# Value rows of the context's experts gathered beside the latents' DeltaNet, from a queue of their own

## The chip, the cores and the metric

The program runs on one NeuronCore of a Trainium2. The metric is the device time of one execution in microseconds. The engines run in parallel, each in its own order: PE (TensorE, matmuls), DVE (VectorE), ACT (ScalarE), POOL (GpSimd, which issues the gathers here) and SP (which issues the other DMAs). They wait for each other by semaphores.

## The reference

A two-layer backbone over 512 latent tokens and 256 context tokens of width 1024. Layer 0 mixes tokens with a gated DeltaNet, layer 1 with attention; each is followed by product-key experts (`peer`), which pick 8 x 16 of 16384 experts for every token:

```python
def block_fn(xb):                      # 128 tokens
    ...
    idx = jnp.take_along_axis(cand_i, pos, axis=-1)      # 128 experts per token
    gate = jax.nn.softmax(best_s, axis=-1)
    act = jax.nn.gelu(jnp.einsum('pd,phkd->phk', xb, u_tab[idx]))
    coef = gate * act
    return jnp.einsum('phk,phkd->pd', coef, v_tab[idx])
...
for i in range(DEPTH):
    ...
    if i % 2 == 0:
        yc, yl = deltanet_mixer(hc, hl, ...)
    else:
        yc, yl = attention_mixer(hc, hl, ...)
    xl = xl + g1l * yl
    xl = xl + g2l * peer(norm(xl), ...)
    if not last:
        xc = xc + g1c * yc
        xc = xc + g2c * peer(norm(xc), ...)
return rmsnorm(xl, final_g)
```

In the DeltaNet the latents start from the state that the context leaves. The context reads nothing of the latents, and its experts' result is needed in layer 1's attention only.

## The kernel before, in words

The order of layer 0 is: the DeltaNet's projections, its steps for the context, the context's output projection and routing, then the DeltaNet of the latents (`dn_rec("l")`), their output projection (`dn_out("l")`), their routing, the table of gates (`gates_build`), a dense pass, and layer 1's attention.

`dn_rec("l")` works in four groups of two heads. A group prepares its chunks (kk, rp), inverts their triangular matrices together (`dn_inv`, in PSUM tiles mg), runs four steps per head and direction (`dn_step`: ks, yr, su, ops, each needing the state that the step before left), and transposes the result (tp), scaled by the gates zt. `dn_out("l")` adds up 16 heads in PSUM (po) for two blocks of 128 tokens at a time, evicts (y) and normalizes them.

Three of the four blocks of latents are not gathered: `dense` evaluates all experts for them, in 128 steps of matmuls (up, y). The fourth block of latents and both blocks of the context are gathered, one row of 128 x 1024 floats (512 KB) at a time, by indirect DMAs that POOL issues:

- `gather_u`: for each of 128 picks the rows of `u` for 128 tokens (L965), and the dot products with the tokens on DVE (L967). After 128 of them a block's coefficients are complete.
- `gather_v`: the values of 64 tokens of the context, one token at a time (L1017), and two matmuls (L1020) that add 128 rows, weighted, into a row of PSUM (yp). A half block is 64 of them, and there are four halves, 256 rows. Ahead of a half the picks and coefficients are transposed on PE (L1004).
- `gather_vt`: the values of the block of latents, summed on DVE (L984).

They share four buffers ("row"). All are generators in one list, `k.bg`. The loops of the main work call `tick(w)` at fixed places, with w from the table RATE, and tick runs a step of the list's first generator for each full unit of credit. So the list's order is the gathers' order: the dot products of the context (256, queued ahead of `dn_rec("l")`), three halves of the context's values (NVA = 3, queued after `dn_out("l")`), then, as routing of the fourth block ends, its dot products and values, and the fourth half. What is left runs in attention (`drain`), before the context is read. From the traced program a scheduler then writes each engine's order.

Of the kernel before, what the change touches and what calls it, by code (L numbers as in the profile page):

```python
# [18 lines left out]
P = 128  # L19
# [12 lines left out]
AHEAD = [i for r in (0, 2, 1, 3) for i in range(r, PK, 4)]      # blocks of experts, in the order of their evaluation ahead  # L32


class Kern:
    def __init__(self, ctx, tc, I, out, dbg):
        self.ctx, self.tc, self.nc, self.I, self.out, self.dbg = ctx, tc, tc.nc, I, out, dbg or {}
        nc = self.nc
        self.bg, self.credit = [], 0.0
        self.ug, self.ucredit, self.nu = None, 0.0, 0  # L40
# [13 lines left out]
    # gathers are issued in small steps between the other work  # L54
    def tick(self, w):
        self.credit += w
        while self.credit >= 1.0 and self.bg:
            self.credit -= 1.0
            try:
                next(self.bg[0])  # L60
            except StopIteration:
                self.bg.pop(0)
        if not self.bg:
            self.credit = 0.0

# [56 lines left out]
    def ada(self, l, r, pool=None):  # L122
        """chunks 2 * r and 2 * r + 1 of a layer's modulations, for latents (row 0) and context (row 1)"""
# [24 lines left out]
    def mod_rows(self, pool, l, s, sub, norm, nb=1, pool_g=None, **kw):  # L148
        """A = norm_g*(1+scale), S = shift, as rows on all partitions"""
# [10 lines left out]
    def norm_mod(self, pool, x, A, S, h):  # L160
        """h <- rmsnorm(x) * A + S"""
# [8 lines left out]
    def transp_split(self, pp, tag, h, hi, lo, b):  # L170
        """h [128, 1024] -> hi/lo[:, kb, b*128:...]"""
# [10 lines left out]
    # tokens on the free axis: 0..511 latents, 512..767 context  # L182
    def gate_math(self, p, pp, gx, n, G):
# [23 lines left out]
        # log1p(e) = ln(u) * e / (u - 1), or e where u rounds to 1  # L207
# [30 lines left out]
    def dn_in(self, G, later, ast, rec):  # L238
        """q, k, v, z and the gates; rec's first step is traced before the last heads, beside which it runs"""
# [67 lines left out]
    def dn_qkv(self, G, p, pp, pwp, hi, lo, wtile, heads, nb):  # L307
# [4 lines left out]
        W2 = TL + 4 + TC          # conv output span: latents, gap of 4, context  # L312
        XC = TL + 6               # start of the context in the padded row
# [83 lines left out]
    def dn_z(self, p, pp):  # L397
        """2 * silu(z)^T of the latents"""
# [24 lines left out]
    def dn_rec(self, seq, G, og_d, st_d):  # L423
# [5 lines left out]
        with ExitStack() as st:  # L429
# [8 lines left out]
            for g0 in range(0, QH, GR):  # L438
                pks, Pss, Us = [], [], []
                pg = p if g0 // GR % 2 else pq  # L440
                for hh in range(GR):
                    h = g0 + hh
                    Ps = pg.tile([P, MH, 2, P], F32, name="Pm", bufs=GR)
                    U = pg.tile([P, MH, 2, P], F32, name="U", bufs=GR)     # (c, v), dir
# [5 lines left out]
                    for c in range(n):  # L450
                        self.tick(self.rate[0])
                        kk = pqp.tile([P, 2, P], F32, name="kk")
                        nc.tensor.matmul(kk.rearrange("p a b -> p (a b)"), pk[:, c, 0, :],
                                         pk[:, c, 0:2, :].rearrange("p a b -> p (a b)"), start=True, stop=True)
                        km = pq.tile([P, 2, 2, P], F32, name="km", bufs=2)     # (kk, kq), dir
                        nc.vector.tensor_mul(km, kk.unsqueeze(2).to_broadcast([P, 2, 2, P]), self.tri.unsqueeze(1).to_broadcast([P, 2, 2, P]))
                        rp = pqp.tile([P, 2, 2, P], F32, name="rp")
                        ar = pq.tile([P, 2, 2, P], F32, name="ar", bufs=2)     # (v, dir)
# [116 lines left out]
    def dn_inv(self, p, pp, Us, MH, Z64):  # L575
        """Us[head][:, m, dir] <- (I + U)^-1, U triangular (upper for dir 0, lower for dir 1)."""
# [23 lines left out]
        R1 = t4("R1", [P, 2 * M, 32])     # rows of the inverses' transposes  # L600
        R2 = t4("R2", [P, 2 * M, 32])     # rows of the inverses
# [9 lines left out]
        # (source, target) blocks  # L611
        pairs = [[(0, 1), (2, 3)], [(1, 0), (3, 2)]]
        tp = pp.tile([P, M, 32], F32, name="mg")
# [5 lines left out]
        Tc = p.tile([P, M, 32], F32, name="Tc")  # L619
        nc.scalar.copy(Tc, tp)  # L620
        self.tick(self.rate[9])
        zp = pp.tile([P, M, 32], F32, name="mg")
# [7 lines left out]
        yp = pp.tile([P, M, 32], F32, name="mg")  # L630
# [13 lines left out]
        T6 = p.tile([P, M, 64], F32, name="T6")  # L644
        for mh in range(2):
            tp = pp.tile([P, 8, 64], F32, name="mg")
# [7 lines left out]
        for mh in range(2):  # L654
            yp = pp.tile([P, 8, 64], F32, name="mg")
# [12 lines left out]
    def dn_out(self, seq, og_d, xin, xout, put):  # L668
        """xout[b] = xin[b] + g1 * (o @ w_out); put(b, rows) for every finished block"""
# [4 lines left out]
        with tc.tile_pool(name="dno", bufs=1) as p, tc.tile_pool(name="dnop", bufs=1, space=PS) as pp:  # L674
# [4 lines left out]
            for b0 in range(0, n, 2):  # L679
                bs = range(b0, b0 + 2)  # L680
                ps = {(b, h): pp.tile([P, 512], F32, name="po", bufs=6 if n > 2 else 4) for b in bs for h in range(2)}
# [21 lines left out]
    def attention(self, xl, xc, order, rows, A0, gst, ost, pst):  # L703
        """(softmax(q k^T) v)^T of the latents, split, by heads; context is read after the gathers that finish it"""
# [533 lines left out]
def body(ctx, tc, I, out, dbg=None, upto=99):  # L1238
# [74 lines left out]
    for i in range(NVA):  # L1313
        vctx(i // 2, i % 2)
# [128 lines left out]
```

## Time and profile before

| | us |
|---|---|
| median of 3 runs (4876.7 to 4892.4) | 4885.92 |
| the profiled execution: span of its instructions | 4891.1 |
| PE busy | 4329.9 |
| DVE busy | 3587.0 |
| POOL busy | 1321.5 |

The profiled execution's own time is not among the runs by name; its span, from the first to the last instruction, lies 5.2 us above the median and 1.3 below the highest run. Busy times of different engines overlap. Most of the program is bound by PE; the stages that matter here are those between 940 and 3360 us of the span.

### The profile page before, as it was taken

How to read it: one execution, taken by the hardware profiler on the slowest of the kernel's cores; microseconds unless marked ns; L12 is line 12 of the kernel's file. 1: busy time of each engine (PE TensorE's matmuls, PEld its weight loads, DVE VectorE, ACT ScalarE, POOL GpSimd, SP SyncE). 2: the span in 40 equal slices, each digit the busy share in tenths (PEclk: the TensorE clock that was granted, in tenths of full speed). 3: DMA queues.
4: the chain of work that ended last, by engine and by line, in shares of the span. 5: the costliest groups of instructions: out<-in, count | busy, mean ns of one | idle time of the engine just before them, and what ended most of it. 6: DMA issues, size and time to landing. Idle time of an engine off the chain costs nothing. (4 is left out here: it accounts for less than half of the span.)

```text
span 4891.1 us, 68996 instructions
## 1 busy us (share of the span) xinstructions
PE 4329.9 (89%) x24564; PEld 3455.1 (71%) x24564; DVE 3587.0 (73%) x8483; ACT 1866.5 (38%) x3605; POOL 1321.5 (27%) x1111
## 2 busy tenths in 40 slices
PE   6999669757569698999999999988997999999998
PEld 3778547545444556666788888745687998888887
DVE  4667825899965857566688888645579888888886
ACT  2335553447450213344333333223333554333333
POOL 0000000134344433222333334440000102444441
PEclk8999789768679899999999999999999999999999
DMA  7744246447578877777999999872133678999996
GB/s 296 261 150 135 75 144 191 153 148 254 177 242 317 301 240 268 269 260 272 329 349 351 339 339 337 292 268 74 61 112 107 215 260 287 355 334 335 336 324 230
DMA packets 480616, 1196.55 MB, mean 245 GB/s; under 512 B 40752, under 2 KB 239152, under 8 KB 470416
## 3 DMA queue, kind: packets, MB, share of 16 engines
q1 hardware_dynamic: 332816, 655.21, 38.2%
q0 software_dynamic: 147456, 536.94, 31.5%
q8 instruction: 194, 3.18, 0.3%
q14 instruction: 150, 1.23, 0.1%
HBM read 1079.50 MB, written 112.49 MB: 244 GB/s over the span
## 5 line engine op out<-in xcount | busy, mean ns | idle before, releaser
L965 POOL DMA_INDIRECT row<-in_peer_u,idx x512 | 613.2, 1198 | 1513.3 <-DVE row L967 706.3
L100 PE MATMUL up<-hil,uh 128*128 128x384 f32 x2048 | 709.4, 346 | 44.7 <-ACT c L1094 44.1
L102 PE MATMUL up<-hil,ul 128*128 128x384 f32 x2048 | 697.2, 340 | 0.0
L101 PE MATMUL up<-lol,uh 128*128 128x384 f32 x2048 | 696.1, 340 | 0.0
L100 PE MATMUL y<-vh,ch 128*128 128x512 f32 x1536 | 602.8, 393 | 9.1 <-ACT ch L106 7.6
L101 PE MATMUL y<-vl,ch 128*128 128x512 f32 x1536 | 602.9, 393 | 0.0
L102 PE MATMUL y<-vh,cl 128*128 128x512 f32 x1536 | 508.8, 391 | 0.0
L981 POOL DMA_INDIRECT row<-in_peer_v,idx x256 | 339.9, 1328 | 456.3 <-DVE lhs L984 374.5
L100 PEld LDWEIGHTS up<-hil,uh 128*128 128x128 f32 x2048 | 386.9, 189 | 94.8 <-ACT c L1094 65.4
L106 ACT CAST uh<-ur 128x1024 fp32r<-128x1024 f32 x256 | 268.3, 1048 | 454.3 <-PE up L101 322.3
L1017 POOL DMA_INDIRECT row<-in_peer_v,iT x256 | 279.5, 1092 | 557.7 <-PE yp L1020 473.7
L107 DVE TENSOR_TENSOR vl<-vr,vh 128x1024 fp32r<-128x1024 f32 x256 | 312.9, 1224 | 127.1 <-ACT vh L106 125.1
L106 ACT CAST vh<-vr 128x1024 fp32r<-128x1024 f32 x256 | 268.6, 1051 | 359.9 <-PE y L102 325.0
L101 PEld LDWEIGHTS up<-lol,uh 128*128 128x128 f32 x2048 | 387.1, 189 | 19.2 <-issue 10.9
L102 PEld LDWEIGHTS up<-hil,ul 128*128 128x128 f32 x2048 | 386.5, 189 | 18.2 <-issue 15.1
L107 DVE TENSOR_TENSOR ul<-ur,uh 128x1024 fp32r<-128x1024 f32 x256 | 312.1, 1220 | 74.7 <-ACT uh L106 70.1
L967 DVE SCALAR_TENSOR_TENSOR row<-row,ghs 128x1024 f32<-128x1024 f32 x256 | 311.2, 1222 | 73.7 <-DMA row<-in_peer_u,idx 72.7
L1066 DVE TENSOR_SCALAR A<-iotar,kt 128x128 f32<-128x128 f32 x768 | 221.8, 289 | 174.4 <-PE gp L1068 171.9
L100 PEld LDWEIGHTS y<-vh,ch 128*128 128x128 f32 x1536 | 289.8, 189 | 70.3 <-ACT ch L106 9.1
L102 PEld LDWEIGHTS y<-vh,cl 128*128 128x128 f32 x1536 | 288.6, 188 | 64.6 <-issue 4.2
L984 DVE SCALAR_TENSOR_TENSOR lhs<-row,lcf,lhs 128x1024 f32<-128x1024 f32 x254 | 325.1, 1280 | 9.6 <-DMA row<-in_peer_v,idx 8.0
L101 PEld LDWEIGHTS y<-vl,ch 128*128 128x128 f32 x1536 | 290.1, 189 | 56.3 <-issue 2.5
(397 smaller groups left out, 8788.1 us busy)
## 6 DMA issues: line engine op xcount, KB each, us to landing
ur<-in_uT SPq DMA_DIRECT2D x256, 512.0 KB
vr<-in_peer_v SPq DMA_DIRECT2D x256, 512.0 KB
w<-in_ada_w SPq DMA_DIRECT2D x48, 1024.0 KB
G_d<-st SPq DMA_DIRECT2D x10, 4096.0 KB
gt<-G_d SPq DMA_DIRECT2D x64, 640.0 KB
act_d<-c SPq DMA_DIRECT2D x129, 192.0 KB
c<-act_d SPq DMA_DIRECT2D x129, 192.0 KB
wr<-in_dn_w_in SPq DMA_DIRECT2D x48, 512.0 KB
```

The source lines that it names most:

```text
L100: first = mm(ps, lh, rh, start=start, stop=False)
L101: mm(ps, lh, rl, start=False, stop=False)
L102: mm(ps, ll, rh, start=False, stop=stop)
L106: self.nc.scalar.copy(hi, src)
L107: self.nc.vector.tensor_sub(lo, src, hi)
L965: nc.gpsimd.indirect_dma_start(out=u, out_offset=None, in_=self.I["peer_u"], in_offset=bass.IndirectOffsetOnAxis(ap=ix[:, k:k + 1], axis=0))
L967: mv = nc.vector.scalar_tensor_tensor(u, u, 1.0, hs, op0=ALU.mult, op1=ALU.mult, accum_out=coef[:, k:k + 1])
L981: nc.gpsimd.indirect_dma_start(out=v, out_offset=None, in_=self.I["peer_v"], in_offset=bass.IndirectOffsetOnAxis(ap=ix[:, k:k + 1], axis=0))
L984: keep(nc.vector.scalar_tensor_tensor(y, v, coef[:, k:k + 1], y, op0=ALU.mult, op1=ALU.add))
L1017: nc.gpsimd.indirect_dma_start(out=v, out_offset=None, in_=self.I["peer_v"], in_offset=bass.IndirectOffsetOnAxis(ap=iT[:, t:t + 1], axis=0))
L1066: nc.vector.tensor_scalar(A, iota, kt[:, 0, t:t + 1], None, op0=ALU.is_equal)
```

## The change

A second list, `k.bgv`, holds the four halves of the context's values. `tick` runs it beside the first one, with credit of its own, and only while the first half's block stands in `summed`, where `gather_u` enters a block after its last dot product:

```diff
+        self.vcredit += w * self.vrate
+        while self.vcredit >= 1.0:
+            self.vcredit -= 1.0
+            if not (self.bgv and self.bgv[0][0] in self.summed):
+                self.vcredit = 0.0
+                break
+            try:
+                next(self.bgv[0][1])
+            except StopIteration:
+                self.bgv.pop(0)
...
         nc.scalar.activation(coef, coef, AF.Gelu)
         nc.vector.tensor_mul(coef, coef, gate.rearrange("p h k -> p (h k)"))
+        self.summed.add(j)
...
-NVA = 3         # halves of context blocks whose values are gathered before those of the latents
+VRATE = 1.0
```

The halves are queued before the latents' DeltaNet. After `dn_out("l")` what is left of them is moved to `k.bg`, ahead of the gathers of the latents; none comes after these:

```diff
+        gat.open_v(gst)
         for b in range(NX) if upto > 1 else ():
             gat.u(0, b, gate[1, b], idx[1, b])
+            for s in range(2):
+                gat.v_half(b, idx[1, b], (0, 1, 5), rows(xm_c, b), rows(xo_c, b), s)
+        k.vrate = VRATE
         for _ in k.dn_rec("l", G, og_l, st_d):
             pass
...
-    gat.open_v(gst)
     k.dense_open(lst, 0, ND, hi, lo)
-    vctx = lambda b, s: gat.v_half(b, idx[1, b], (0, 1, 5), rows(xm_c, b), rows(xo_c, b), s)
-    for i in range(NVA):
-        vctx(i // 2, i % 2)
+    k.vrate = 0.0
+    k.bg += [g for _, g in k.bgv]
+    k.bgv = []
...
     k.routing(0, hi, lo, TL, *lat, order, gathers)
-    for i in range(NVA, 2 * NX):
-        vctx(i // 2, i % 2)
...
-    k.drain(2 * NX - NVA)
+    k.drain()
```

The buffers of `gather_v` are so open during the DeltaNet, and others are made smaller: kk and mg share one PSUM bank, Tc and T6 one buffer, the latents' zt has two buffers in place of four, the latents' output projection five accumulators in place of six, and the copy cT falls away:

```diff
-                        kk = pqp.tile([P, 2, P], F32, name="kk")
+                        kk = pqp.tile([P, 2, P], F32, name="kk", tag="kk")
...
-        tp = pp.tile([P, M, 32], F32, name="mg")
+        tp = pp.tile([P, M, 32], F32, name="mg", tag="kk")
...
-        T6 = p.tile([P, M, 64], F32, name="T6")
+        T6 = p.tile([P, M, 64], F32, name="T6", tag="T6", bufs=1)
...
-                ps = {(b, h): pp.tile([P, 512], F32, name="po", bufs=6 if n > 2 else 4) for b in bs for h in range(2)}
+                ps = {(b, h): pp.tile([P, 512], F32, name="po", bufs=5 if n > 2 else 4) for b in bs for h in range(2)}
...
-        cT = pv.tile([P, P], F32, name="cT")
-        nc.vector.tensor_copy(cT, yp[:, 0:P])
...
-ZT = 8, 4
+ZT = 8, 2
```

Comments are taken out too, so line numbers after are some ten higher (L1031 after is L1020 before, L702 is L690, L997 is L984).

The first place is PE's order in the steps of the latents' last DeltaNet group. Before:

```order
L529 MATMUL ks<-S,pk 128x256 x2
L564 MATMUL ops<-vn,Pm 128x128 x2
L540 MATMUL yr<-pk,U 128x128
L529 MATMUL ks<-S,pk 128x256 x2
L541 MATMUL yr<-R,U 128x128
L540 MATMUL yr<-pk,U 128x128
L541 MATMUL yr<-R,U 128x128
L564 MATMUL ops<-vn,Pm 128x128 x4
```

and after, where `yp<-row,Cz` is a gathered value row of the context:

```order
L1031 MATMUL yp<-row,Cz 32x512 x2
L541 MATMUL ks<-S,pk 128x256 x2
L562 MATMUL su<-vd,pk 128x256
L576 MATMUL ops<-vn,Pm 128x128 x2
L552 MATMUL yr<-pk,U 128x128
L553 MATMUL yr<-R,U 128x128
L552 MATMUL yr<-pk,U 128x128
L553 MATMUL yr<-R,U 128x128
L1031 MATMUL yp<-row,Cz 32x512 x2
```

Before, no gathered value stood in this group; after, a pair of matmuls for one stands between one step and the next.

The second place is PE's order in the latents' output projection, from the last step on. Before:

```order
L564 MATMUL ops<-vn,Pm 128x128 x2
L513 MATMUL tp<-ident,o 128x128 x16
L690 MATMUL po<-W,o 128x512 x95
L176 MATMUL tr<-ident,fh 128x128 x8
L690 MATMUL po<-W,o 128x512 x11
L176 MATMUL tr<-ident,fh 128x128 x8
L690 MATMUL po<-W,o 128x512 x22
L1004 MATMUL yp<-ident,gcf_6341 128x128
L176 MATMUL tr<-ident,fh 128x128 x8
```

and after:

```order
L576 MATMUL ops<-vn,Pm 128x128 x2
L1031 MATMUL yp<-row,Cz 32x512 x4
L525 MATMUL tp<-ident,o 128x128 x16
L702 MATMUL po<-W,o 128x512 x26
L1031 MATMUL yp<-row,Cz 32x512 x2
L702 MATMUL po<-W,o 128x512 x3
L1031 MATMUL yp<-row,Cz 32x512 x2
L702 MATMUL po<-W,o 128x512 x4
L1031 MATMUL yp<-row,Cz 32x512 x2
L702 MATMUL po<-W,o 128x512 x26
L1031 MATMUL yp<-row,Cz 32x512 x2
```

Value rows now stand between the projection's matmuls (po), and before they began behind them, with the transposes of the coefficients (gcf).

The third place is DVE's order at the end of the dense pass, where lhs is the gathered block of latents and rt the dense blocks' results. Before (the first piece, and a little later the second):

```order
L984 SCALAR_TENSOR_TENSOR lhs_12955<-row,lcf_12956,lhs_12955 128x1024
L107 TENSOR_TENSOR vl<-vr,vh 128x1024
L984 SCALAR_TENSOR_TENSOR lhs_12955<-row,lcf_12956,lhs_12955 128x1024
L991 TENSOR_TENSOR lhs_12955<-lhs_12955,row 128x1024
L107 TENSOR_TENSOR ul<-ur,uh 128x1024
L1121 TENSOR_TENSOR c<-c,gt 128x320
L1122 TENSOR_TENSOR c<-c,st 128x64
L992 TENSOR_TENSOR lhs_12955<-lhs_12955,row 128x1024
```

```order
L1121 TENSOR_TENSOR c<-c,gt 128x320
L1122 TENSOR_TENSOR c<-c,st 128x64
L107 TENSOR_TENSOR cl<-c,ch 128x384
L1155 TENSOR_TENSOR rt__27332<-y_20097,dg_27328 128x512
L1155 TENSOR_TENSOR rt__27332<-y_20098,dg_27328 128x512
L1156 TENSOR_TENSOR rt__27332<-rt__27332,rx 128x512
L1155 TENSOR_TENSOR rt__27340<-y_20099,dg_27328 128x512
L1156 TENSOR_TENSOR rt__27332<-rt__27332,rx 128x512
```

and after:

```order
L997 SCALAR_TENSOR_TENSOR lhs_13120<-row,lcf_13121,lhs_13120 128x1024
L119 TENSOR_TENSOR cl<-c,ch 128x384
L997 SCALAR_TENSOR_TENSOR lhs_13120<-row,lcf_13121,lhs_13120 128x1024 x3
L1166 TENSOR_TENSOR rt__27324<-y_20604,dg_27320 128x512
L1166 TENSOR_TENSOR rt__27324<-y_20605,dg_27320 128x512
L1166 TENSOR_TENSOR rt__27332<-y_20606,dg_27320 128x512
L1166 TENSOR_TENSOR rt__27332<-y_20607,dg_27320 128x512
L997 SCALAR_TENSOR_TENSOR lhs_13120<-row,lcf_13121,lhs_13120 128x1024
L1167 TENSOR_TENSOR rt__27324<-rt__27324,rx 128x512 x2
L1167 TENSOR_TENSOR rt__27332<-rt__27332,rx 128x512 x2
L997 SCALAR_TENSOR_TENSOR lhs_13120<-row,lcf_13121,lhs_13120 128x1024 x3
```

Before, the latents' gathered values were complete ahead of the last dense steps; after, the last of them stand behind the first evictions of the dense results.

## Rows read from the trace of the kernel before

**Rows 1.** The page's first lines: span, then busy time and instructions of each engine

```profile
span 4891.1 us, 68996 instructions
...
PE 4329.9 (89%) x24564; PEld 3455.1 (71%) x24564; DVE 3587.0 (73%) x8483; ACT 1866.5 (38%) x3605; POOL 1321.5 (27%) x1111
```

**Rows 2.** Windows of six stages: engine busy us (instructions), TensorE clock, DMA share, GB/s

```profile
core 0: us, PE busy (x) PEld busy (x) DVE busy (x) ACT busy (x) POOL busy (x), PEclk, DMA share, GB/s
940.00:1285.00 345.00, 201.51 (x2220) 159.24 (x2222) 316.59 (x749) 199.96 (x635) 128.59 (x113) 0.69 0.59 198
1285.00:1450.00 165.00, 120.81 (x1190) 99.90 (x1186) 133.43 (x308) 104.57 (x369) 74.70 (x67) 0.82 0.65 216
1450.00:1627.00 177.00, 120.68 (x295) 55.54 (x294) 105.97 (x174) 9.36 (x17) 84.06 (x70) 0.82 0.87 310
1627.00:2332.00 705.00, 660.90 (x3449) 455.63 (x3449) 468.50 (x1824) 236.35 (x306) 233.92 (x211) 0.98 0.78 267
2332.00:3183.00 851.00, 849.13 (x4062) 726.57 (x4062) 672.07 (x974) 294.65 (x395) 330.11 (x281) 1.00 0.92 334
3183.00:3360.00 177.00, 145.15 (x614) 83.75 (x610) 81.39 (x187) 47.99 (x153) 63.29 (x64) 0.90 0.60 206
```

**Rows 3.** Windows of three stages, PE records of L1020 alone: PE, PEld, clock, DMA

```profile
1627.00:2332.00 705.00, 188.40 (x740) 25.96 (x740) 0.98 0.78 267
2332.00:3183.00 851.00, 24.77 (x100) 3.47 (x100) 1.00 0.92 334
3183.00:3360.00 177.00, 43.91 (x188) 6.06 (x184) 0.90 0.60 206
```

**Rows 4.** PE timeline in routing: start us, us, operation, records

```profile
1799.69 0.33 PE L101 MATMUL up<-lol,uh 128*128 128x384 f32 x1
1799.95 1.05 PE L1020 MATMUL yp<-row,Cz 128*32 128x512 f32 x4
1800.93 0.44 PE L102 MATMUL up<-hil,ul 128*128 128x384 f32 x1
1801.21 0.33 PE L100 MATMUL up<-hil,uh 128*128 128x384 f32 x1
1801.38 0.34 PE L101 MATMUL up<-lol,uh 128*128 128x384 f32 x1
```

**Rows 5.** PE timeline at the end of the dense pass, two value rows

```profile
3182.44 1.05 PE L1020 MATMUL yp<-row,Cz 128*32 128x512 f32 x4 [0.29 <-DMA row<-in_peer_v,iT]
3189.84 1.92 PE L1020 MATMUL yp<-row,Cz 128*32 128x512 f32 x4 [6.34 <-DMA row<-in_peer_v,iT]
```

**Rows 6.** Waits of PE in 1627 to 2332: us in total, times, longest

```profile
PE yp L1020 <- DMA row<-in_peer_v,iT: 32.0, 14, 7.2
```

**Rows 7.** Waits of PE in 3183 to 3360

```profile
PE yp L1020 <- DMA row<-in_peer_v,iT: 12.5, 7, 6.3
PE pa L100 <- DVE qn L761: 6.2, 2, 3.6
```

**Rows 8.** PE timeline of the latents' output projection

```profile
1465.58 84.79 PE L690 MATMUL po<-W,o 128*128 128x512 f32 x190 [13.52 <-DMA W<-in_dn_w_out]
...
1561.40 19.05 PE L690 MATMUL po<-W,o 128*128 128x512 f32 x44
1599.32 0.47 PE L1004 MATMUL yp<-ident,gcf 128*128 128x128 f32 x1 [18.87 <-DVE y L697]
...
1627.82 0.80 PE L100 MATMUL qp<-hil,qwh 128*128 128x512 f32 x1 [7.96 <-ACT qwh L106]
```

**Rows 9.** DVE timeline there: the second pair's first eviction

```profile
1589.18 0.69 DVE L697 TENSOR_TENSOR y<-po,g 128x512 f32<-128x512 f32 x1
```

**Rows 10.** One window, POOL's u gathers (L965) alone: busy (instructions), clock, DMA

```profile
1475.00:1500.00 25.00, 10.53 (x12) 1.00 1.03 406
```

**Rows 11.** Window at the start of the dense pass, all engines (columns of rows 2)

```profile
2380.00:2580.00 200.00, 200.00 (x966) 176.09 (x965) 171.65 (x290) 73.14 (x98) 80.28 (x70) 1.00 0.96 353
```

**Rows 12.** The page's group of POOL's value gathers: busy, mean ns, idle before

```profile
L1017 POOL DMA_INDIRECT row<-in_peer_v,iT x256 | 279.5, 1092 | 557.7 <-PE yp L1020 473.7
```

More of the change, by code (lines that the diff above doesn't have):

```diff
@@ L39, in __init__ @@
         self.bg, self.credit = [], 0.0
+        self.bgv, self.vcredit, self.vrate, self.summed = [], 0.0, 0.0, set()
         self.ug, self.ucredit, self.nu = None, 0.0, 0
@@ L618, in dn_inv @@
                     nc.tensor.matmul(tp[sl(t), m], U[sl(s), k, d, sl(t)], Zc[d][sl(s), m], start=True, stop=True, tile_position=(32 * s, 32 * t))
-        Tc = p.tile([P, M, 32], F32, name="Tc")
+        Tc = p.tile([P, M, 32], F32, name="Tc", tag="T6", bufs=1)
         nc.scalar.copy(Tc, tp)
         self.tick(self.rate[9])
-        zp = pp.tile([P, M, 32], F32, name="mg")
+        zp = pp.tile([P, M, 32], F32, name="mg", tag="kk")
         for m in range(M):
@@ L629, in dn_inv @@
         self.tick(self.rate[9])
-        yp = pp.tile([P, M, 32], F32, name="mg")
+        yp = pp.tile([P, M, 32], F32, name="mg", tag="kk")
         for m in range(M):
@@ L643, in dn_inv @@
         self.tick(self.rate[9])
-        T6 = p.tile([P, M, 64], F32, name="T6")
+        T6 = p.tile([P, M, 64], F32, name="T6", tag="T6", bufs=1)
         for mh in range(2):
-            tp = pp.tile([P, 8, 64], F32, name="mg")
+            tp = pp.tile([P, 8, 64], F32, name="mg", tag="kk")
             for mm in range(8):
@@ L654, in dn_inv @@
         for mh in range(2):
-            yp = pp.tile([P, 8, 64], F32, name="mg")
+            yp = pp.tile([P, 8, 64], F32, name="mg", tag="kk")
             for mm in range(8):
@@ L955, in routing, with gather_u @@
                     done(b)
-    def gather_u(self, l, p, hs, gate, idx, coef):
+    def gather_u(self, l, p, hs, gate, idx, coef, j):
         nc = self.nc
@@ L1007, in gather_v @@
         nc.vector.tensor_copy(iT, yp[:, P:2 * P])
-        cT = pv.tile([P, P], F32, name="cT")
-        nc.vector.tensor_copy(cT, yp[:, 0:P])
         Cd = Cz.rearrange("p (g q) -> p g q", g=2)[:, :, 0:32 * 32:33]
-        nc.vector.tensor_copy(Cd, cT[:, 64 * s:64 * s + 64].rearrange("p (g i) -> p g i", g=2))
+        nc.vector.tensor_copy(Cd, yp[:, 64 * s:64 * s + 64].rearrange("p (g i) -> p g i", g=2))
         yp = pp.tile([P, 512], F32, name="yp")
@@ L1210, in u @@
         k = self.k
-        k.bg.append(k.gather_u(l, self.p, self.hs[j], gate, idx, self.coef[j]))
+        k.bg.append(k.gather_u(l, self.p, self.hs[j], gate, idx, self.coef[j], (l, j)))
     def v(self, j, idx, g2row, xin, put):
@@ L1218, in v_half @@
         k = self.k
-        k.bg.append(k.gather_v(self.p, self.pv, self.pp, self.Cz, self.coef[j], idx, g2row, xin, xout, s))
+        k.bgv.append(((0, j), k.gather_v(self.p, self.pv, self.pp, self.Cz, self.coef[j], idx, g2row, xin, xout, s)))
 class Rows:
```

## The prediction

> **What bounds the kernel now.** I began with the page's head: 4891.1 us of span, TensorE (PE) busy in 4329.9 of it [rows 1]. So PE's idle time is some 560 us altogether, and a change that only moves work can give back no more than what it puts into that idle time. The median of the runs shown is 4885.9 us, 5.2 below this profiled execution's span; I take differences from the trace and add them to the median. The runs lie 16 us apart, so 0.3% (15 us) is about what a measurement of this kernel tells from no change.
>
> The second view is a table of stages [rows 2]: the last group of the latents' DeltaNet (1285 to 1450), the output projection (1450 to 1627), routing with the gates (1627 to 2332), the dense pass (2332 to 3183), and the start of attention (3183 to 3360); its first row is the DeltaNet groups before. PE's idle time is the stretch less its busy time: 44 us in the last group, 56 in the projection, 44 in routing, 2 in the dense pass and 32 in attention's start. The dense pass is bound by PE, and every microsecond that PE gets there shows in the end. In the DeltaNet stages PE waits for a chain of small steps, and work can hide.
>
> The third view is the same table for the value gathers' matmuls alone [rows 3]. A gathered row leaves four records, so 740, 100 and 188 records are 185, 25 and 47 rows: those are the places which the change empties or fills. POOL gathers 256 of them at 1092 ns each [rows 12].
>
> **What a row costs PE.** In routing a row stands between matmuls whose starts lie 0.17 us apart (1801.21 to 1801.38). From the matmul before it to the third after it, 1799.69 to 1801.38, are 1.69 us, where three steps of 0.17 would be 0.51 [rows 4]. So a row takes 1.18 us of a busy PE; its record alone says 1.05. At the end of the dense pass the same record is 1.05 once and 1.92 the next time, after PE had waited 6.34 us [rows 5]; at the low clock I take 2.0 with what lies around it.
>
> **Term A, the last DeltaNet group: +36 rows.** By the order on PE, about 36 rows come between the coefficients of the first block and the end of this group, 16 beside the triangular inversion and 18 between the steps (two more behind them). The inversion waits for other engines, and I cost its rows at nothing: PE's 44 idle us cover 36 rows at 1.18 (42 us) just about. Between steps a row may stand before the matmul that the chain waits for; I charge half of the 18, 18 x 1.18 x 0.5 = 11 us. The shared places (kk and mg in one bank, Tc and T6 in one buffer, two zt buffers in place of four) can each hold a step back; no row prices them, and I add 4 us, about 1 for each of the four groups. A = **+15**. From below 0, all hidden; from above every row in full at the low clock, 36 x 2.0 = 72, and the 4 rounded up, 77. I choose the lower part, because the granted clock is 0.82 in this stage and not at its low level throughout [rows 2].
>
> **Term B, the output projection: +24 rows.** 24 x 1.18 = 28 us of PE. PE waits 13.52 us for W at the start; its last 44 matmuls take from 1561.40 to 1580.45; then it waits 18.87 us for the eviction of the second pair (L697) before 1599.32, and routing's first matmul starts at 1627.82 [rows 8]. So 47 us lie between the last projection matmul and routing. DVE reaches that eviction at 1589.18 only, 9 us after the matmul, since it stands behind gathered dot products [rows 9]. By the order on DVE the second pair's evictions come 29 dot products earlier than before (186 instead of 215), at the pace of 12 in 25 us [rows 10] some 60 us of work that is not ahead of them; I take 20 us off the tail, which is the 9 and part of the normalizing that follows. B = 28 - 20 = **+8**. Bounds: -20 if all rows fall into the waits; +28 if the tail stays; with five accumulators instead of six PE can stop for the first pair as it does for the second, 18.87 more, +47.
>
> **Term C, routing and the gates: -28 rows.** By the order 157 in place of 185. -28 x 1.18 = -33. Against it stands a coupling. Before, all of the context's dot products were through early in routing, and the value rows then had the four buffers for themselves; PE waited 32.0 us for them in 14 waits [rows 6]. Now POOL issues a value row and a u row by turns well into routing, and each needs one of the same four buffers: a value row waits for DVE to have done the u row ahead of it, and a u row for PE. I put a third of the present 32, 12 us rounded up, on top. C = **-21**; from below -33, from above 44 idle us doubled, -33 + 44 = +11.
>
> **Term D, the dense pass: +17 rows.** By the order 39 rows instead of 22. PE has no idle time there, so 17 x 1.18 = +20. The latents' own gathers start some ten mix steps later as well and are denser afterwards. The early part runs at a DMA share of 0.96 and 353 GB/s [rows 11], the pass as a whole at 0.92 and 334 [rows 2], which is 363 at a full share, so a gather of 512 KB takes 1.44 us. 17 more are 24 us, against 8% of 851, 68 us, that are free; +3 for the crowded beginning. D = **+23**; without the DMA's part +20, and with a quarter of the 24 us late, +26, rounded up to +29.
>
> One rule speaks against the 3. The Trainium skill (DMA: Bandwidth & Descriptors, Specifications) gives a limit of about 358 GB/s of HBM for one core. By it the early dense pass, at 353, is full, and what is added stretches it: estimated from that page, 7 more gathers in 100 us want 390 GB/s, and some 9 us would be lost. This trace moved 406 GB/s in a window of the projection [rows 10], so here the measurement disagrees with the page, and I keep 3; by the page the sum below would be 6 us higher.
>
> **Term E, attention's start: no rows instead of 47.** -47 x 1.18 = -55, and the 12.5 us that PE waits for their data go too [rows 7]. Not all of that is won. PE waits 6.2 us for qn there already [rows 7], and with the filler gone the chain of norms behind it shows: +12, twice that wait. And the last six of the latents' value rows now end after the dense evictions (before: five mix steps earlier), while attention takes the gathered block first; at 25 us for 12, 2.1 us each [rows 10], that is +12. E = -55 - 12 + 12 + 12 = **-43**; from below -67 without the last two, from above -30 when the chain shows 13 more.
>
> The copy of cT that is left out is four DVE instructions of 128x128 off PE's path, nothing; if DVE was late for them, a few tenths of a microsecond each.
>
> **The sum.** 15 + 8 - 21 + 23 - 43 = -18 us, 4885.9 - 18 = **4868**. Its own range is 4840 to 4885: -46 if A and B's halves hide, 0 if C's coupling eats its gain.
>
> **Rivals.**
>
> *All of it hides.* The idle PE in A takes the rows at nothing, B's are in its waits (-20), C is -33, D +20, E -55: -88, **4798**. For it speaks that 44 + 56 us of idle PE face 60 rows at 1.18, 71 us [rows 2]; against it, that an in-order engine takes a row where it stands, not where it idles.
>
> *It only moves.* Every row costs its full price wherever it lands, and the tail of B stays as long: 42 + 28 - 33 + 20 - 55 = +2, **4888**, no change. For it speaks that PE is 89% busy over the whole kernel [rows 1], and that the tail in B has a normalizing chain that no reordering of the dot products shortens. Here the change does what it says and gains nothing.
>
> *The last group slows down.* The rows between steps each stop the chain at the low clock: A = +77, the others as forecast, +44, **4930**. The place is the four steps of the last group, where a value row stands between one step's matmul and the next step's; its price 2.0 us [rows 5]. It decides from the point where A passes 48 us, which is the forecast's 15 and the 33 to the bound of slower (18 + 15). For it speaks the clock of 0.82 and the 0.69 of the groups before [rows 2]; against it, that more work on PE between the steps is also less idling, and the 1.92 of rows 5 came after a wait.
>
> **Chances.** Forecast 0.4, all hidden 0.2, only moved 0.2, slower group 0.2. The forecast's range lies two thirds below 4871 (faster by over 0.3%): faster 0.27, same 0.13. All hidden is faster, 0.2. Only moved gives 0.04, 0.10 and 0.06. The slower group is slower, 0.2. Together faster 0.51, same 0.23, slower 0.26. The range goes to both outer cases, 4795 to 4932.
>
> **What would show it.** In the changed kernel's trace the last DeltaNet group should be 10 to 20 us longer than its 165, with value rows in it; the gap between the last projection matmul and routing's first some 27 us instead of 47; routing and gates about 20 us shorter; the dense pass some 23 longer, still without idle PE; and no value matmul in attention, whose start is some 43 shorter. The prediction is wrong if the last group grows by 50 or more, if routing grows because value and u rows wait for each other, or if the dense pass becomes bound by the gathers.

## The result, and the profile after

The changed kernel takes 4966.07 us (median of 4 runs, 4948.07 to 4969.91), the kernel before 4887.03 in the same comparison: a ratio of 1.0154, interval 1.0133 to 1.0175. It is slower by 79 us, where 18 faster were forecast and the range ended at 4932. One execution of all, 10198 us of `ks1_half05`, fell in a slower state and is left out of that kernel's ratio.

The page's head of the changed kernel answers to [rows 1]. PE does almost the same work as before (4343.5 us busy, 4329.9 before), so 63 of the 77 us between the two spans are PE's idle time:

```profile
span 4968.1 us, 68921 instructions
...
PE 4343.5 (87%) x24564; PEld 3465.0 (70%) x24564; DVE 3587.2 (72%) x8479; ACT 1864.6 (38%) x3605; POOL 1336.1 (27%) x1111
```

To see where, I cut both spans at the same events: **A** from the last step (yr) of the latents' first DeltaNet group to that of the fourth, **B** to routing's first matmul (qp), **C** to the first matmul of the dense pass (y), **D** to its last, **E** to the end. The first group's last step ends at 1098.5 before and at 1098.3 after, so nothing is lost ahead of A. The windows (columns as in [rows 2]) are, before:

```profile
1098.50:1436.10 337.60, 224.27 (x2509) 183.61 (x2508) 298.19 (x691) 206.95 (x700) 152.50 (x133) 0.77 0.68 226
1436.10:1627.80 191.70, 126.24 (x311) 58.27 (x310) 110.36 (x184) 21.42 (x67) 89.22 (x74) 0.81 0.83 299
1627.80:2332.45 704.65, 660.90 (x3450) 455.64 (x3450) 468.95 (x1825) 236.03 (x306) 234.16 (x211) 0.98 0.78 267
2332.45:3181.16 848.71, 847.57 (x4054) 726.34 (x4058) 671.46 (x972) 292.39 (x391) 328.62 (x279) 1.00 0.92 334
3181.16:4891.10 1709.94, 1588.79 (x7929) 1344.93 (x7929) 1298.72 (x3140) 647.18 (x990) 421.06 (x330) 0.97 0.67 236
```

and after:

```profile
1098.30:1526.80 428.50, 266.79 (x2642) 191.51 (x2640) 318.68 (x732) 206.49 (x698) 182.59 (x166) 0.74 0.66 218
1526.80:1726.80 200.00, 153.44 (x413) 60.50 (x413) 65.59 (x108) 21.27 (x63) 70.06 (x61) 0.86 0.76 264
1726.80:2412.90 686.10, 637.15 (x3339) 452.93 (x3339) 512.95 (x1903) 235.45 (x306) 253.45 (x223) 0.98 0.82 283
2412.90:3285.10 872.20, 868.42 (x4116) 727.51 (x4116) 658.56 (x955) 292.25 (x391) 351.57 (x289) 1.00 0.92 328
3285.10:4968.10 1683.00, 1545.89 (x7733) 1343.75 (x7733) 1309.83 (x3153) 649.35 (x990) 380.84 (x287) 0.96 0.64 227
```

So A grew by 90.9 us, B by 8.3, C shrank by 18.6, D grew by 23.5, and E, to the end of the span, shrank by 27. The loss is A. Two things are to be seen in it. The first is in PE's timeline around the third group's inversion (mg) and the fourth group's kk. Before, the fourth group's kk run from 1204.78, long ahead of the third group's last mg; its own mg starts at 1348.02:

```profile
1204.78 0.70 PE L453 MATMUL kk<-pk 128*128 128x256 f32 x2 [3.68 <-DMA pk<-pk_d]
...
1243.20 1.22 PE L453 MATMUL kk<-pk 128*128 128x256 f32 x2 [2.65 <-DVE km L456]
...
1293.67 1.97 PE L660 MATMUL mg<-U,T 64*64 64x64 f32 x32
...
1348.02 0.62 PE L618 MATMUL mg<-R,U 32*32 32x32 f32 x48 [1.75 <-DVE R L603]
```

After, they start at 1308.22, right behind the third group's last mg, in whose bank they now lie, and the fourth inversion starts 61 us later than before, at 1408.67:

```profile
1303.34 1.97 PE L672 MATMUL mg<-U,T 64*64 64x64 f32 x32
...
1308.22 0.60 PE L465 MATMUL kk<-pk 128*128 128x256 f32 x2
...
1338.07 0.60 PE L465 MATMUL kk<-pk 128*128 128x256 f32 x2
...
1408.67 0.74 PE L630 MATMUL mg<-R,U 32*32 32x32 f32 x36 [0.91 <-DVE R L615]
```

The second is PE's waits from the third group's end to the last step (1361 to 1527; us in total, times, longest). The largest is for gathered rows:

```profile
PE yp L1031 <- DMA row<-in_peer_v,iT: 27.0, 14, 4.8
```

### The profile page after: what moved, and what is told of

Its sections match the earlier page's. It is cut to its first block, busy times and chain, and to the rows that moved or that the text cites. A ratio compares the mean times of both kernels' runs of the same rounds, so it can differ in the third digit from the quotient of the medians.

```text
span 4968.1 us, 68921 instructions
## 1 busy us (share of the span) xinstructions
PE 4343.5 (87%) x24564; PEld 3465.0 (70%) x24564; DVE 3587.2 (72%) x8479; ACT 1864.6 (38%) x3605; POOL 1336.1 (27%) x1111
## 5 line engine op out<-in xcount | busy, mean ns | idle before, releaser
L977 POOL DMA_INDIRECT row<-in_peer_u,idx x512 | 602.5, 1177 | 1533.2 <-DVE row L979 626.7
L994 POOL DMA_INDIRECT row<-in_peer_v,idx x256 | 351.9, 1375 | 427.1 <-DVE lhs L997 362.1
L1028 POOL DMA_INDIRECT row<-in_peer_v,iT x256 | 292.1, 1141 | 539.5 <-PE yp L1031 348.9
L1031 PE MATMUL yp<-row,Cz 128*32 128x512 f32 x1024 | 277.3, 642 | 68.8 <-DMA row<-in_peer_v,iT 63.8
L997 DVE SCALAR_TENSOR_TENSOR lhs<-row,lcf,lhs 128x1024 f32<-128x1024 f32 x254 | 325.4, 1281 | 12.8 <-DMA row<-in_peer_v,idx 11.0
```

The source lines that it names most:

```text
L977: nc.gpsimd.indirect_dma_start(out=u, out_offset=None, in_=self.I["peer_u"], in_offset=bass.IndirectOffsetOnAxis(ap=ix[:, k:k + 1], axis=0))
L994: nc.gpsimd.indirect_dma_start(out=v, out_offset=None, in_=self.I["peer_v"], in_offset=bass.IndirectOffsetOnAxis(ap=ix[:, k:k + 1], axis=0))
L997: keep(nc.vector.scalar_tensor_tensor(y, v, coef[:, k:k + 1], y, op0=ALU.mult, op1=ALU.add))
L1028: nc.gpsimd.indirect_dma_start(out=v, out_offset=None, in_=self.I["peer_v"], in_offset=bass.IndirectOffsetOnAxis(ap=iT[:, t:t + 1], axis=0))
L1031: nc.tensor.matmul(yp[sl(2 * g + j), :], Cz[:, (32 * g + i) * 32:(32 * g + i + 1) * 32], v[:, j * 512:(j + 1) * 512], start=i == 0, stop=i ...
```

## The experiments

All times are medians; a difference is to the kernel before in the same comparison, a ratio is given with its interval. This table cuts every kernel's profiled execution at the events above. Behind a time stands the number of the context's value rows on PE in that stretch (records of their matmuls by four); "left" are the latents' value rows on DVE after the dense pass.

| kernel | A | B | C | D | E | left |
|---|---|---|---|---|---|---|
| before | 337.6 | 191.7 | 704.6 / 185 | 848.7 / 23 | 1709.9 / 49 | 0 |
| changed | 428.5 / 34 | 200.0 / 26 | 686.1 / 157 | 872.2 / 39 | 1683.0 / 0 | 6 |
| b_room | 380.1 | 196.5 | 691.8 / 184 | 847.1 / 23 | 1702.7 / 50 | 0 |
| b_kkmg | 374.4 | 189.3 | 701.2 / 185 | 853.4 / 24 | 1707.0 / 48 | 0 |
| a_rp | 344.8 / 14 | 217.0 / 36 | 685.0 / 140 | 903.9 / 66 | 1714.7 / 0 | 23 |
| a_late | 380.7 | 195.8 / 26 | 713.9 / 157 | 910.2 / 73 | 1735.0 / 0 | 33 |
| a_half | 425.5 / 34 | 196.9 / 26 | 703.1 / 132 | 906.7 / 64 | 1665.3 / 0 | 0 |
| a_ks1 | 341.6 / 15 | 213.2 / 35 | 691.9 / 140 | 900.3 / 66 | 1717.4 / 0 | 25 |
| a_vr05 | 405.6 / 18 | 202.8 / 18 | 685.9 / 156 | 899.5 / 64 | 1710.0 / 0 | 20 |
| b_out | 335.8 | 190.8 / 26 | 715.0 / 157 | 850.7 / 24 | 1712.2 / 50 | 0 |
| b_nva4 | 343.1 | 191.1 | 700.2 / 185 | 908.8 / 71 | 1725.6 / 0 | 31 |
| ks1_half | 342.6 / 15 | 211.3 / 35 | 675.0 / 140 | 858.5 / 28 | 1698.6 / 39 | 0 |
| b_out05 | 342.1 | 209.3 / 19 | 676.0 / 163 | 845.9 / 23 | 1713.4 / 52 | 0 |
| b_gb3 | 369.6 | 195.8 | 654.9 / 148 | 886.5 / 44 | 1821.7 / 64 | 24 |
| b_room4 | 379.9 | 194.1 | 694.3 / 184 | 914.6 / 72 | 1727.7 / 0 | 31 |
| ks1_half05 | 335.4 / 9 | 221.4 / 26 | 690.7 / 156 | 847.5 / 24 | 1707.4 / 42 | 0 |

### The room-making alone, and one bank alone

`b_room` is the kernel before with the last diff of the section on the change and nothing else; `b_kkmg` takes of it only

```diff
-                        kk = pqp.tile([P, 2, P], F32, name="kk")
+                        kk = pqp.tile([P, 2, P], F32, name="kk", tag="kk")
...
-        tp = pp.tile([P, M, 32], F32, name="mg")
+        tp = pp.tile([P, M, 32], F32, name="mg", tag="kk")
...
```

> The kernel before with all the room-making of the change (kk and mg in one bank, Tc and T6 in one buffer, two zt buffers, five accumulators, no cT), and its old queue: the value rows stay behind the output projection. Sharing theory (the lookahead of the DeltaNet groups is lost, since the next group's kk can only start when this group's mg is through): about 60 us slower than before, some 4945, with the last step of the fourth group about 60 us later and kk of each group starting right after mg of the one before. Rows theory (value rows between the steps stop the chain): 0 to 5 us from before, 4885 to 4892.

> The kernel before with nothing but kk and mg in one PSUM bank. Sharing theory: the same 60 us as with all the room-making, within 10. Rival (another of the shared places, such as the zt buffers or T6, holds the groups back): under 10 us from before.

Measured: 4924.66 (1.0083, 1.0057 to 1.011) and 4928.85 (1.009, 1.0061 to 1.012), so 37 and 41 us slower, less than the 60 expected. A is 380.1 and 374.4 without a single value row in it:

```profile
1099.00:1473.40 374.40, 215.74 (x2504) 180.87 (x2503) 320.41 (x735) 204.81 (x696) 152.99 (x134) 0.73 0.62 205
```

That is 37 us over before, at a busy PE that is 9 us shorter: the chain of the groups has come apart. One bank explains the whole of it; the zt buffers, T6 and the accumulators together can't be told from nothing. In `b_kkmg` too, the fourth group's kk start right behind the third group's last mg:

```profile
1301.36 1.97 PE L660 MATMUL mg<-U,T 64*64 64x64 f32 x32
...
1305.92 0.60 PE L453 MATMUL kk<-pk 128*128 128x256 f32 x2
```

### Another bank instead: kk with rp, or one ks

```diff
-                        kk = pqp.tile([P, 2, P], F32, name="kk", tag="kk")
+                        kk = pqp.tile([P, 2, P], F32, name="kk", tag="rp")
...
-        tp = pp.tile([P, M, 32], F32, name="mg", tag="kk")
+        tp = pp.tile([P, M, 32], F32, name="mg")
...
```

> The changed kernel, but kk shares its bank with rp, and mg has one of its own; value rows run beside the DeltaNet as in the change. Sharing theory: 60 of the 79 us come back, about 4900 (4890 to 4915), and what is left of the loss in the last group is the rows' own, some 27 us. Rows theory: at most 15 come back, 4950 or more.

`a_ks1` gives kk, rp and mg a bank each and takes one of the latents' two ks.

```diff
-            ks = pp.tile([P, 2, 2, P], F32, name="ks", bufs=2)
+            ks = pp.tile([P, 2, 2, P], F32, name="ks", bufs=2 if first else 1)
```

> The changed kernel, but kk and mg have a bank each, and the bank for the value rows comes from the steps (one ks instead of two). Lookahead theory: the first group ends as before (about 1098), and from there to the last group's last step it takes 340 to 365 us instead of 428, value rows included. What that is worth in the end depends on the gathers: with about 20 value rows fewer in the DeltaNet (15 by PE's order, not 34) the latents' values end later, so the dense pass and the start of attention give back 30 to 60 us, as with kk and rp in one bank: in all 4930 to 4975. If the second ks bank is needed by the steps, the DeltaNet stays above 400.

Measured: 5008.53 (1.0256, 1.0217 to 1.0295) and 4963.99 (1.0154, 1.0134 to 1.0173). In both, A is back near 340, value rows included:

```profile
1103.50:1445.10 341.60, 236.82 (x2541) 181.99 (x2540) 274.32 (x647) 206.26 (x701) 145.80 (x129) 0.80 0.65 213
1445.10:1658.30 213.20, 163.32 (x450) 60.11 (x449) 74.55 (x122) 20.41 (x60) 83.82 (x79) 0.86 0.80 283
```

So mg's own bank is what the groups need in A, and a second ks is not. With kk and rp together the first group came 41 us later (its last step ends at 1139.7), which I had not expected: the kk of the first two groups take from 953.5 to 1047.0 there, and from 936.6 to 986.9 in the kernel before. The 87 us won in A with one ks, as expected, vanish again: the dense pass takes 900.3, and 25 rows of the latents are left behind it. My expectation for `a_rp`, that 60 us come back, was wrong, and the reasons are the 41 us ahead of A, and D and E, which are 63 us longer than in the changed kernel.

### No rows beside the DeltaNet, or half as many

```diff
-        k.vrate = VRATE
         for _ in k.dn_rec("l", G, og_l, st_d):
             pass
+        k.vrate = VRATE
```

> The changed kernel with its shared places, but the second queue starts only with the output projection (no value rows beside the DeltaNet's steps). Sharing theory: the DeltaNet stays 60 us too long, and about 36 rows move to routing at up to 1.2 us each: 4945 to 4985. Rows theory: the DeltaNet is as short as before, 4870 to 4900.

```diff
-VRATE = 1.0
+VRATE = 0.5
```

> The changed kernel with the second queue at half its rate (18 value rows by the end of the steps instead of 34, by PE's order). Theory that rows in the last group cost about 1.35 us each there (PE waits in its order for their data): the last group is 15 to 25 us shorter than in the change. Theory that the 48 us there come from something that one row or 36 cause alike: it stays within 8 us. The whole: 4935 to 4975, since the rows come later.

Measured: 5035.17 (1.0312, 1.0275 to 1.0348) and 5008.87 (1.0256, 1.0231 to 1.0281), both slower than the changed kernel. A is 380.7 with no rows, 405.6 with 18 and 428.5 with 34, a straight line of 1.4 us per row; the last group is 145.2 us long with half the rate and was 165.1, 20 us less, as expected. Without rows A stays 43 us above before, where I expected 60. The totals are not as expected, against 4945 to 4985 and 4935 to 4975: what A wins, the later stages lose more than once over.

### The fourth half's place

`a_half` puts the fourth half behind the latents' gathers again; `b_nva4` puts it ahead of them in the kernel before, with no other edit:

```diff
-NVA = 3
+NVA = 4
```

> The changed kernel, but the fourth half of the context's values stands behind the latents' gathers again, as before the change. Theory of the late latents (each value row of the latents that is left when the dense pass ends holds attention's first block up by about 2 us, while one of the context's costs attention about 0.6): no latent row is left at the end of the dense pass, the dense pass gives back most of its 23 us, attention's start takes some 40 context rows again, and the sum is 8 to 30 us below the changed kernel, 4936 to 4958; the DeltaNet stays as long as in the change. Rival (where the fourth half stands doesn't matter, since every row costs PE the same 1.2 us wherever it lands): within 8 us of the changed kernel.

> The kernel before with one number changed: all four halves of the context's values stand ahead of the latents' gathers (NVA = 4), as in the change, and none beside the DeltaNet. Theory of the one stream (the gathers run one after the other through four buffers at some 3 us each, so 64 that are moved ahead push the latents' values past the end of the dense pass, where each costs about 2.1 us, and one of the context's 0.9): 40 to 55 latent rows are left there, the dense pass has some 65 context rows more and the sum is 60 to 140 us above before, 4945 to 5025. Rival (there is room in the stream, and the fourth half's place is worth little): within 25 us of before.

Measured: 4999.52 (1.0233, 1.0215 to 1.0251) and 4982.27 (1.0203, 1.0181 to 1.0225). The second total is as expected: this one line costs 97 us. Its parts are smaller than I put them (some 65 context rows more in the dense pass, 40 to 55 latent rows left behind it). D has 48 context rows more than before, and PE's busy time there grows by 57 us, 1.2 a row. Then 31 rows of the latents are left, and attention, which takes that block first, waits. PE's longest wait in the 90 us from the dense pass's end on is, in the view of waits,

```profile
PE tr L176 <- issue: 75.3, 1, 75.3
```

in that kernel, and in the changed one, in the timeline, with 6 rows left,

```profile
3311.19 1.94 PE L188 MATMUL tr<-ident,hrow 128*128 128x128 f32 x8 [26.12 <-issue]
```

that is 49 us for 25 rows, 2.0 each. The records call it issue. Ahead of it stands DVE's sum of those rows; in DVE's timeline of `b_nva4` its last product and its last addition (lhs) are

```profile
3307.05 1.28 DVE L984 SCALAR_TENSOR_TENSOR lhs<-row,lcf,lhs 128x1024 f32<-128x1024 f32 x1 [0.35 <-DMA row<-in_peer_v,idx]
...
3310.54 1.23 DVE L992 TENSOR_TENSOR lhs<-lhs,row 128x1024 f32<-128x1024 f32 x1
```

and the norm of the block, from which the transposes (tr) are made, comes behind them. In the changed kernel that addition starts at 3305.09. The first kernel, `a_half`, refutes what I expected: no latent row is left, E is the shortest of all at 1665.3, yet the kernel is 32 us slower than the changed one. The latents are now so early that 38 of their dot products run in routing, where PE waits 27.6 us for DVE in the table of gates (its waits from 1717 to 2420, below), and all 64 rows of the fourth half fall into the dense pass:

```profile
PE gp L1079 <- DVE B L1078: 27.6, 34, 1.1
```

### Both undone, and the queue beside the projection alone

`ks1_half` is `a_half` with the banks of `a_ks1`; `ks1_half05` is that with VRATE 0.5.

> The changed kernel with both losses taken away at once: kk and mg have a bank each (one ks in place of two), and the fourth half stands behind the latents' gathers. Theory (the two add up: the groups' lookahead, and the latents being late): routing starts at about 1658 as with the banks alone, no latent row is left at the end of the dense pass, in all 4890 to 4945, still no better than before, since the value rows only take the places of dot products in the stream. If rows beside the DeltaNet were a gain of their own, as I had forecast: below 4875.

> The kernel with a bank each for kk and mg, one ks and the fourth half late, at half the second queue's rate. Theory (value rows displace dot products in one stream): with 9 rows instead of 15 by the end of the steps the projection is a few us shorter and routing a few longer, 4885 to 4915. If rows beside the DeltaNet are a gain in this order too, fewer of them are a loss: 4920 or more.

Measured: 4914.69 (1.0066, 1.0042 to 1.0091) and 4910.4 (1.0048, 1.0032 to 1.0064). The profiled execution of the first was its shortest run, 4887.83, so its row of the table lies 27 us below its median. Both are within what was expected: the two costs are gone, some 50 of the 79 us with them, and neither rate makes the kernel better than before.

`b_out` keeps the DeltaNet of before and opens the second queue only behind it, the fourth half late; `b_out05` does so at half the rate. Of the edit only the opening of the queue is shown; the projection keeps the change's five accumulators:

```diff
+    gat.open_v(gst)
+    for b in range(NX):
+        for s in range(2 - b):
+            gat.v_half(b, idx[1, b], (0, 1, 5), rows(xm_c, b), rows(xo_c, b), s)
+    k.vrate = VRATE
     hi, lo, hs, coef = ffn_pool(k, lst, NL - ND)
```

> The second queue beside the output projection alone: the DeltaNet is that of the kernel before, with its banks and buffers; the queue opens behind it, and the fourth half stays behind the latents' gathers. Theory (the loss is the DeltaNet's and that of the late latents): the DeltaNet ends as before, the projection grows by 0 to 10 us, routing loses 0 to 25, and the sum is 4870 to 4892. Rival (the two queues side by side are themselves slower, since value rows and dot products wait for each other's buffers): routing and the dense pass grow together by 20 us or more, 4905 or later.

> The kernel with the second queue beside the projection alone, at half its rate. With it in full the projection was no longer and routing some 10 us longer though 28 value rows had left it. Theory (every value row in the projection displaces a dot product, which then runs in routing between value rows): about half of the 13 to 26 value rows there, routing 700 to 712 us, in all 4895 to 4915. Rival (the loss is not a matter of how many rows): 4915 or more.

Measured: 4917.93 (1.0065, 1.0048 to 1.0083) and 4885.17 (1.0001, 0.9984 to 1.0019). With 26 rows the projection costs nothing, but routing takes 715.0 us though 28 rows have left it, and PE waits 47.0 us there for value rows, where it was 32.0 [rows 6]:

```profile
PE yp L1031 <- DMA row<-in_peer_v,iT: 47.0, 11, 11.1
```

That is the rival's total, though routing and the dense pass grew by 12 us together and not by 20. Of the 20 us between the two profiled spans 8 lie ahead of A (the first group ends at 1107.0, and at 1098.5 before), ahead of where the second queue opens; why is not known. With 19 rows it is the kernel before again, better than I expected (4895 to 4915), the best of the versions with a second queue, and no gain. Its parts are not those of the theory: the projection is 17.6 us longer than before with fewer rows, and routing takes 676.0 and not 700 to 712. So the number of rows alone does not set what they cost there.

### What paces the gathers, and whether the costs add up

```diff
-GB = 4
+GB = 3
```

> The kernel before with three shared buffers for gathered rows in place of four. Theory that the four buffers set the pace of the gathers from the DeltaNet to attention (POOL waits for one to come free): in the DeltaNet and the projection, where 190 dot products run from the end of the first group to routing, at most 165 do, and the kernel is 40 us or more slower. Theory that the steps' credit or DVE sets the pace: 180 or more, and within 20 us.

Measured: 5020.93 (1.0275, 1.0252 to 1.0298), 136 us slower, as the theory of the four buffers says. But 112 of the 136 lie in E, where 64 rows of the context and 24 of the latents stand; A and B grew by 36 together. The number of dot products there does not agree with the theory: 182 of 190. The stretch grew with them, to 565 us, so one gather takes 3.1 us in place of 2.8, far from a third more. In A alone it is 124 dot products in this kernel, and in every other one without value rows there, though A takes from 336 us (`b_out`) to 381 (`a_late`): there the program's order sets their number. The buffers are a part of the pace, not all of it.

`b_room4` is `b_room` with NVA = 4: both costs, no second queue.

> The kernel before with everything of the change but the second queue: all the room-making, and all four halves ahead of the latents' gathers. Alone the two cost 37 and 97 us. If they add up, 5015 to 5035, and the changed kernel's 4966 says that its value rows beside the DeltaNet and the projection are worth 50 to 70 us in that order of gathers. If they overlap (a later DeltaNet gives the gathers time, so that fewer latent rows are left), 4960 to 5000, and the rows are worth little.

Measured: 5009.1 (1.0268, 1.0237 to 1.03), 124 us slower, a little under the 134 of the two alone. So they nearly add up, and against this kernel the value rows of the second queue are worth 45 us: 124 less 79. With the fourth half behind the latents they are a loss of 74 (`a_half`, 111 over before, against `b_room`, 37). The rows have no price of their own; it depends on what is late behind them.

## Why the prediction was wrong

**Term A is the step that failed**: 15 us forecast, 77 as its bound, 90.9 measured. Three things in it were wrong. The first is the stage. I read 1285 to 1450 in [rows 2] as the last group, but the third group's last step ends at 1345.4 and the fourth's at 1436.1, so that window holds a part of the third. The last group alone is

```profile
1345.40:1436.10 90.70, 64.73 (x805) 53.85 (x803) 72.62 (x154) 58.16 (x199) 47.62 (x41) 0.83 0.75 250
```

and PE is idle there for 26 us and not for 44, too few for 36 rows at 1.18. The changed kernel's last group, 165.1 us, is therefore 74 longer, although the prediction gave 165 for the kernel before.

The second is a term that was mis-sized. For the shared places I put 4 us, "about 1 for each of the four groups"; one bank for kk and mg costs 37 to 43 in A, because it takes away that a group is prepared ahead, during the inversion of the one before. I thought of a step held back, and not of what is done ahead across groups.

The third is the rows' price. "The inversion waits for other engines, and I cost its rows at nothing", and I charged 11 us for those between the steps: against `b_room`, which has the same banks, the inversion's stretch is 23 us longer and that of the steps 25. The pairs of windows show it, first the changed kernel:

```profile
1408.60:1460.70 52.10, 35.27 (x570) 15.67 (x572) 21.55 (x45) 10.53 (x25) 28.94 (x27) 0.63 0.81 259
1460.70:1526.80 66.10, 58.20 (x326) 37.85 (x324) 34.60 (x77) 31.70 (x113) 36.75 (x35) 0.97 0.82 274
```

and the room-making alone:

```profile
1407.00:1436.20 29.20, 17.42 (x522) 15.52 (x523) 22.60 (x47) 10.56 (x26) 19.25 (x15) 0.51 0.71 231
1436.20:1476.80 40.60, 38.45 (x252) 32.82 (x250) 32.36 (x77) 30.24 (x111) 14.31 (x16) 1.00 0.65 211
```

PE had 12 us to spare in the inversion, and the rows did not go into them: its busy time is 17.9 us longer there and its idle time 5.0, and in the steps 19.8 and 5.7. So a row costs its matmuls in full, and a part of the wait for its data. It stands in PE's order whether these have come or not, and the inversion's next matmul stands behind it, as PE's timeline of the changed kernel shows (columns as in [rows 4]):

```profile
1422.26 1.92 PE L1031 MATMUL yp<-row,Cz 128*32 128x512 f32 x4 [3.99 <-DMA row<-in_peer_v,iT]
1424.11 0.63 PE L638 MATMUL mg<-Tc,R 32*32 32x32 f32 x26
...
1434.69 3.20 PE L1031 MATMUL yp<-row,Cz 128*32 128x512 f32 x8 [4.76 <-DMA row<-in_peer_v,iT]
```

The rival with the slower last group came nearest and named half of the mechanism: rows that stop the chain. Its price was off too: 2.0 us a row, from the low clock, where 1.4 were measured, with a granted clock of 0.63 on the mean in the inversion and of 0.97 in the steps. That its 77 lies near the 90.9 is luck, since it had the bank at 4 as well.

**Term B was right**: +8 forecast, +8.3 measured, and in its parts. PE's busy time grew by 27.2 (28 forecast), and the gap from the last projection matmul to routing fell from 47.4 to 28.9 us (20 less were forecast).

**Term C was right in sum**, -21 against -18.6, and partly by luck, since two errors offset each other. PE's busy time fell by 23.8 and not 33, so a row there was worth some 0.85 us, less than the 1.18 read between dense matmuls; its idle time grew by 5, not 12. The coupling that I put the 12 for does not show: PE's wait for value rows fell from 32.0 us [rows 6] to 21.9. What grew is its wait for ACT's c; the first line is of the kernel before, the others are of the changed one:

```profile
PE up L100 <- ACT c L1094: 8.4, 9, 2.6
...
PE yp L1031 <- DMA row<-in_peer_v,iT: 21.9, 15, 5.1
PE up L112 <- ACT c L1105: 21.1, 19, 2.8
```

**Term D was right**, +23 against +23.5, with 16 rows more at 1.3 us of busy time each. The Trainium skill's limit of about 358 GB/s of HBM for one core (DMA: Bandwidth & Descriptors, Specifications), which I had set aside, would have shown as a dense pass that waits for data. The pass moved 328 GB/s, and PE's idle time in it grew by 2.6 us. That does not test the limit, since the crowded beginning, for which I had added 3 us, did not come about: the stretch that answers to [rows 11] moved 304 GB/s where it was 353, and the 3 us that PE is idle are in it:

```profile
2461.00:2661.00 200.00, 196.93 (x895) 146.18 (x892) 114.24 (x188) 58.04 (x78) 74.04 (x64) 0.99 0.88 304
```

**Term E was too large**, -43 against -27. PE's busy time fell by 43 and not by 55 (0.87 us a row). Its idle time grew by 16 where the two terms of 12, less 12 saved, gave 12. The last latent rows were a good guess: with 6 left, attention's first matmul (tr) starts 26.1 us behind the dense pass, and 11.2 before.

What I had not asked is why the stages balance as they do. The gathers share four buffers, and the second queue does not bring more of them through. From A to B before ran 190 dot products in 529 us, 2.8 us a gather; after, 152 dot products and 60 value rows in 628 us, 3.0 a gather. With one ks it was 140 and 50 in 555 us, 2.9: fifty value rows earlier are fifty dot products later. In the changed kernel the stretch is 99 us longer, and 60 value rows still leave 38 dot products to routing. The latents' rows, which have a deadline at the end of the dense pass, come later with them. Moving the fourth half ahead of these, an edit that I counted only as rows in D and E, costs 87 to 97 us by itself without the second queue. So on one path the 79 us are 37 for the room-making, 87 for the fourth half, and 45 won by the rows. On the other they are 37, 74 lost by the rows with the fourth half late, and 32 won by the fourth half's place (`a_half`). With a bank each and one ks that place costs 46 (`a_ks1` against `ks1_half`). Neither the rows nor that place has a price of its own.

Why the rows lose 74 us with the fourth half late is shown as far as the stages go (A +45, C +11, D +60, E -37 against the room-making alone). Of D's 60 us 50 are PE's busy time, 1.2 for each of 41 rows more, and 9 its idle time, first the room-making alone and then `a_half`:

```profile
2365.06:3212.10 847.04, 847.04 (x4053) 726.16 (x4053) 672.67 (x971) 292.51 (x391) 337.42 (x280) 1.00 0.93 335
2420.10:3326.80 906.70, 897.29 (x4216) 728.23 (x4216) 621.45 (x887) 291.80 (x391) 354.20 (x278) 1.00 0.87 312
```

Why rows and fourth half change each other's price is argued from these stages and not tried by itself. Nor was a fifth buffer tried.

## What to carry to other kernels

When two tiles are put into one bank, look in PE's timeline for the first instruction of the next iteration that writes one of them: if it runs before the last one of this iteration on the other, the bank takes away work done ahead, and its price comes from that lead and not from a wait (here kk ran 89 us ahead, and the price was 37 to 43). Idle time of an in-order engine is not free room for work that needs gathered data: charge such work its full time and a part of the wait for its data (1.4 us a row in the chain here, 0.85 in routing, 1.2 to 1.3 in the dense pass). And before moving a part of a stream of gathers ahead, ask which part of the stream has a deadline, and count how many of its pieces will miss it.

## What was not expected of the hardware

With kk and rp in one bank the kk of the first two groups took 94 us in place of 50, and the first group ended 41 us later. From the first group's end to routing a gather takes 2.8 to 3.3 us in all of these kernels, with none to 60 value rows for PE among the dot products for DVE. That is the time divided by the number of gathers, which the program's order sets in part, and not a measured limit.
